# Hybrid encoder layer on Trainium2: one of the two score products of the stick-breaking heads on 64 instead of 128 rows of TensorE

## The chip, the core and the metric

The kernel runs on one core of a Trainium2 chip. The metric is device time of one execution in microseconds (us); lower is better. The engines are called as in the profile: PE is TensorE's matmul side, PEld its weight loads, DVE VectorE, ACT ScalarE, POOL GpSimd, and SP the engine whose queue issues most DMAs.

## What is computed

One encoder layer on a sequence of 2048 positions with 1024 features: a normalisation, a projection to queries, keys and values, two groups of eight heads with 64 features each, an output projection, and an MLP with 4096 hidden features. Only the first group of heads is touched by the change. It is stick-breaking attention, strictly causal, cut here to its core:

```python
z = jnp.einsum('bqhd,bkhd->bhqk', qb, kb).astype(jnp.float32) * scale
strict = s_idx < t_idx
log_beta = jax.nn.log_sigmoid(z)
log_1m_beta = jnp.where(strict, jax.nn.log_sigmoid(-z), 0.0)
suffix = lax.cumsum(log_1m_beta, axis=3, reverse=True) - log_1m_beta
w = jnp.where(strict, jnp.exp(log_beta + suffix), 0.0)
outs.append(jnp.einsum('bhqk,bkhd->bqhd', w.astype(v.dtype), vb))
```

A weight is thus the sigmoid of the score, times the product of the sigmoids of the negated scores of all keys between this key and the query. The second group is softmax attention in a band of keys with a position bias.

## The kernel before

**Numbers in two parts.** PE multiplies operands of type fp32r here. For accuracy each fp32 number is kept as two such parts: the first is the number rounded, the second what the rounding left over (`split`). A product of two matrices is made as first x first, first x second, second x first (`mm3`), added up in PSUM.

**Stages.** Projections of the later half of the sequence come first, to about 420 us. Then comes attention, to about 1360 us, with the rest of the projections and the output projection of finished blocks as filler between its steps. The last stage, the MLP with the remaining output projection, is dense PE work.

**The score tile.** Scores of the heads are made from 64 features, half of PE's 128 rows. The kernel uses the other half for the parts of the keys: `load_k` (line 673) puts the first parts of k on partitions 0 to 63 and the second parts on 64 to 127. `load_q` (line 666) puts the same 64 features of q on both halves; index 0 of its tile is q's first part, index 1 its second. One product over 128 rows therefore gives q's first part times (k's first plus k's second part), and another gives q's second part times the same sum. In `SB.scores` (line 776) the two are added in one PSUM tile `z`, for 128 queries (the loaded weights) by up to 512 keys (the moving columns). In units on the diagonal the keys ahead of the query block are left out, so that 512, 384, 256 or 128 columns remain, and a third product of identity and mask in bf16 writes a large negative number where a key isn't before the query (line 785).

**The steps of a unit.** A unit (`SB`) is a head, a block of 512 queries and a block of 512 keys; there are 80, each with four steps of 128 queries. In a step, `soft1` (line 787) makes two sigmoids on ACT, a running product (scan) along the keys on DVE, and the weights as a product on POOL. Eight steps later (`LAG`, line 1039) the weights are transposed on PE (tiles `wt`), split by ACT and DVE (`wth`, `wtl`), and multiplied with the values (`acc`).

**Order of the work.** PE's order is the program's: all PE calls go through `Ordered`, whose line 42 is therefore the line of nearly all instructions in the profile. The loop at line 1115 goes step by step: transposes of the unit eight steps back, `soft1` of the current step, splits of the transposed weights, products with the values, then the scores of the next step (called ahead by one step), then filler. `fill` (line 1055) gives out filler products (tiles `pf` and `po`) by a credit that grows with the weight of a step, so their share follows the steps and not the clock. Units run from the last query block to the first; in each block the stick-breaking units come ahead of the softmax units. The softmax heads (`CA`) make their scores by the same pair of 128-row products (`cz`, `ct`).

Of the kernel before, what the change touches and what calls it, by code (L numbers as in the profile page):

```python
# [21 lines left out]
HD = 64  # L22
# [57 lines left out]
def encoder_kernel(ctx, tc, xT, c, g1, g2, w_in, w_rest, gqk, bias, w_o, w1, w2, w_ada, b_ada, out):  # L80
    nc = tc.nc
    act, dve, pool, sp = nc.scalar, nc.vector, nc.gpsimd, nc.sync
    pe = Ordered(tc, nc.tensor)
# [572 lines left out]
    if True:  # L656
# [97 lines left out]
        class SB(Unit):  # L754
# [21 lines left out]
            def scores(self, qi):  # L776
                nm = f"{self.nm}_{qi}"
                c0 = qi * P if self.diag else 0
                n = TB - c0
                self.z = z = pz.tile([P, TB], F32, tag="z", name=f"z{nm}")  # L780
                qs = slice(qi * P, (qi + 1) * P)
                pe.matmul(z[:, :n], self.q[:, 0, qs], self.k[:, c0:], start=True, stop=False)
                pe.matmul(z[:, :n], self.q[:, 1, qs], self.k[:, c0:], start=False, stop=not self.diag)
                if self.diag:
                    pe.matmul(z[:, :P], identb, maskb, start=False, stop=True)

# [892 lines left out]
```

## Time and profile before

| | us |
|---|---|
| median of the 2 runs shown | 2668.22 |
| lowest and highest of them | 2667.61, 2668.83 |
| span of the profiled execution | 2672.1 |
| PE busy in it | 2598.4 |
| attention, roughly | 410 to 1360 |
| PE busy in 410 to 1360 | 908.5 of 950 |
| first and last stick-breaking score product | 421.1, 1269.1 |

The span is that of one profiled execution; the profile tells no further time around it, so it stands for that execution's own time, 3.9 us above the median. A row of a group reads: line, engine, operation, output<-inputs by the program's names, shape, count, then busy time in us and the mean duration of one in ns, then the idle time of the engine before these instructions and what ended it. The pair ahead of the shape (128*128) tells the rows and columns of PE that the instruction uses. Busy time counts overlapping instructions once, so busy time over count is nearer to the rate than the duration is. Rows of the timeline read: start in us, length in us, engine, instruction, count, and in brackets an idle time before it. Ends of products are modelled in the records; starts tell the rate.

### The profile page before, as it was taken

The numbers are of one execution on the slowest core, as the hardware profiler recorded it, in microseconds if no ns is written. First come the engines' busy times: TensorE is split into PE (matmuls) and PEld (weight loads), VectorE is DVE, ScalarE is ACT, GpSimd is POOL, SyncE is SP. The second block draws the span as 40 slices with busy tenths as digits, with TensorE's granted clock in tenths as the row PEclk, the third lists the DMA queues.
The fourth block names the chain that finished last, engine by engine and source line by source line (L and its number), as shares of the span: only waits on it lengthen the run. The fifth ranks groups of instructions, "written<-read, shape, count | busy, mean of one in ns | idle before, by whom it ended". The sixth has DMA issues, their size and how long they took to land. (4 is left out here: it accounts for less than half of the span.)

```text
span 2672.1 us, 40291 instructions
## 1 busy us (share of the span) xinstructions
PE 2598.4 (97%) x12944; PEld 2162.5 (81%) x12944; DVE 1929.1 (72%) x3287; ACT 1511.7 (57%) x2962; POOL 919.8 (34%) x1192
## 2 busy tenths in 40 slices
PE   6999999898999999999999999999999999999999
PEld 5888887687878887778788888878888888888887
DVE  7656766698789878989768787677857656555555
ACT  5333436787688878878654444456544545444443
POOL 4330144576467656767522323100002323200000
PEclk9999999999999999999999999999999999999999
DMA  9879888988887687756677777786675343465574
GB/s 339 307 300 363 313 318 261 262 255 258 251 260 249 203 260 251 236 191 206 208 276 274 273 255 266 252 322 221 222 265 175 138 166 140 148 250 197 194 266 156
DMA packets 263061, 651.28 MB, mean 244 GB/s; under 512 B 29632, under 2 KB 61376, under 8 KB 252992
## 3 DMA queue, kind: packets, MB, share of 16 engines
q1 hardware_dynamic: 261552, 643.98, 70.5%
q10 hardware_dynamic: 1296, 4.72, 0.4%
q8 instruction: 103, 1.69, 0.3%
q14 instruction: 110, 0.90, 0.1%
HBM read 457.21 MB, written 191.37 MB: 243 GB/s over the span
## 5 line engine op out<-in xcount | busy, mean ns | idle before, releaser
L42 PE MATMUL ps<-oph,opv 128*128 128x512 f32 x2688 | 612.5, 390 | 0.3
L42 PE MATMUL ps<-h,opw 128*128 128x512 f32 x2664 | 607.0, 390 | 4.3 <-DVE cx L42 4.3
L42 PEld LDWEIGHTS ps<-oph,opv 128*128 128x128 f32 x2688 | 503.8, 188 | 107.0 <-DVE opv L42 1.2
L42 PEld LDWEIGHTS ps<-h,opw 128*128 128x128 f32 x2664 | 500.6, 188 | 110.3 <-DVE cx L42 5.8
L42 POOL TENSOR_TENSOR b<-b,p 128x512 f32<-128x512 f32 (+1 forms) x320 | 360.3, 1126 | 197.9 <-DVE p L42 176.6
L42 DVE TENSOR_TENSOR wtl<-wt,wth 128x512 fp32r<-128x512 f32 (+3 forms) x544 | 290.5, 545 | 52.5 <-ACT wth L42 50.0
L42 ACT CAST wth<-wt 128x512 fp32r<-128x512 f32 (+3 forms) x544 | 257.8, 485 | 118.8 <-PE wt L42 104.0
L42 DVE TENSOR_TENSOR oph<-hw,oph 128x512 fp32r<-128x512 f32 x224 | 156.4, 698 | 220.4 <-ACT oph L42 220.4
L42 ACT CAST oph<-hw 128x512 fp32r<-128x512 f32 x224 | 139.5, 623 | 283.3 <-PE ps L42 267.2
L42 PE MATMUL pt<-w,ht 128*128 128x512 f32 x1248 | 288.7, 391 | 2.2 <-DVE qh L42 2.2
L42 POOL TENSOR_TENSOR ts<-w 128x512 f32<-128x512 f32 x32 | 44.8, 1400 | 668.4 <-DMA w<-in_w_dram 576.7
L42 PEld LDWEIGHTS pt<-w,ht 128*128 128x128 f32 x1248 | 232.8, 188 | 50.5 <-ACT csq L42 2.9
L42 DVE TENSOR_TENSOR_SCAN p<-z,p,zero 128x512 f32<-128x512 f32 x192 | 246.1, 1282 | 34.6 <-ACT z L42 29.2
L42 PE MATMUL acc<-wth,v 128*128 128x512 f32 (+3 forms) x544 | 222.6, 413 | 0.8 <-ACT wth L42 0.8
L42 ACT ACTIVATE b<-z 128x512 f32<-128x512 f32 (+1 forms) x320 | 171.7, 537 | 65.7 <-PE z L42 48.3
L42 PE MATMUL z<-k,q 128*128 128x512 f32 (+3 forms) x640 | 186.5, 373 | 9.7 <-DVE p L42 7.2
L42 POOL TENSOR_TENSOR e<-e,cols 128x640 f32<-128x640 f32 (+4 forms) x128 | 143.2, 1123 | 146.1 <-DVE cols L42 81.3
L42 PE MATMUL acc<-wtl,v 128*128 128x512 f32 (+3 forms) x544 | 187.1, 350 | 0.0
L42 DVE TENSOR_TENSOR opw<-w,opw 128x512 fp32r<-128x512 f32 x127 | 103.8, 819 | 113.1 <-ACT opw L42 113.0
L42 PE MATMUL wt<-ident,b 128*128 128x128 f32 x1088 | 173.3, 275 | 6.8 <-DVE cols L42 5.1
L42 ACT ACTIVATE z<-z 128x512 f32<-128x512 f32 (+1 forms) x320 | 170.4, 532 | 0.0
L42 PEld LDWEIGHTS wt<-ident,b 128*128 128x128 f32 x1088 | 134.8, 142 | 37.9 <-DVE cols L42 6.7
(193 smaller groups left out, 4257.6 us busy)
## 6 DMA issues: line engine op xcount, KB each, us to landing
hw<-scr_hid SPq DMA_DIRECT2D x112, 512.0 KB, 3.9
k<-scr_k SPq DMA_DIRECT2D x272, 128.0 KB, 4.2
v<-scr_v SPq DMA_DIRECT2D x136, 256.0 KB, 4.3
q<-scr_q SPq DMA_DIRECT2D x128, 256.0 KB, 5.4
w<-in_w_dram SPq DMA_DIRECT2D x64, 512.0 KB, 5.2
hw<-scr_s SPq DMA_DIRECT2D x64, 512.0 KB, 4.6
fw<-scr_w SPq DMA_DIRECT2D x28, 1024.0 KB, 7.0
wa<-in_w_ada_dram SPq DMA_DIRECT2D x48, 512.0 KB, 6.3
```

Source lines behind the costliest of these rows:

```text
L42: return lambda *x, **y: self.tc.keep_in_program_order(f(*x, **y))
```

## The change

In `SB.scores`, the second product of each tile takes partitions 0 to 63 alone of both operands: q's second part with k's first part. The lower half of that product, q's second part with k's second part, is no longer computed. The first product, the mask, the loads of q and k on all 128 partitions, and the softmax heads stay as they are.

```diff
                 pe.matmul(z[:, :n], self.q[:, 0, qs], self.k[:, c0:], start=True, stop=False)
-                pe.matmul(z[:, :n], self.q[:, 1, qs], self.k[:, c0:], start=False, stop=not self.diag)
+                pe.matmul(z[:, :n], self.q[0:HD, 1, qs], self.k[0:HD, c0:], start=False, stop=not self.diag)
```

## Prediction

> **What bounds the kernel now.** I read the page of the profile first: busy time by engine, then the groups by shape, which split the page's mixed groups.
>
> ```profile
> PE 2598.4 (97%) x12944; PEld 2162.5 (81%) x12944; DVE 1929.1 (72%) x3287; ACT 1511.7 (57%) x2962; POOL 919.8 (34%) x1192
> ```
>
> TensorE (PE) has work in 97% of the span. That is an average over stages, so the next view is the busy time by stretch, for the stretches in which only stick-breaking units are in front; the changed product occurs nowhere else.
>
> ```profile
> 421.00:481.00 60.00, 55.57 (x324) 43.87 (x322) 45.54 (x86) 47.06 (x119) 38.25 (x70) 0.97 0.93 276
> 527.00:654.00 127.00, 122.76 (x786) 106.14 (x785) 110.02 (x159) 104.32 (x221) 85.37 (x137) 0.99 0.80 247
> 744.00:926.00 182.00, 181.29 (x1157) 157.26 (x1156) 165.06 (x215) 150.42 (x312) 127.00 (x193) 1.00 0.73 232
> 1033.00:1270.00 237.00, 232.58 (x1274) 190.23 (x1273) 213.62 (x262) 192.87 (x381) 179.79 (x259) 0.99 0.68 216
> sum 606.00, PE 592.19 PEld 497.50 DVE 534.24 ACT 494.67 POOL 430.40; mean PE 148.05 PEld 124.37 DVE 133.56 ACT 123.67 POOL 107.60
> ```
>
> The columns after the length are PE, PE's weight loads, DVE, ACT, POOL, the granted clock, DMA share and GB/s. PE is busy 592.2 of 606 us, DVE 534.2 (88%). PE is idle for 13.8 us in all. So nothing on PE is hidden here: a nanosecond more on PE in a step lengthens that step, and up to 72 us of DVE idle time would be what a faster PE could win before DVE bound the stretches.
>
> How many instructions the edit touches, and how long one takes, is in the groups with shapes kept apart:
>
> ```profile
> L42 PE MATMUL z<-k,q 128*128 128x512 f32 x448 | 144.5, 404 | 6.6 <-DVE p L42 6.3 <-DMA k<-scr_k 0.2
> L42 PE MATMUL z<-k,q 128*128 128x384 f32 x64 | 16.7, 342 | 0.0
> L42 PE MATMUL z<-k,q 128*128 128x256 f32 x64 | 13.5, 294 | 1.7 <-DVE cols L42 1.3 <-DVE p L42 0.2
> L42 PE MATMUL z<-k,q 128*128 128x128 f32 x64 | 12.0, 268 | 1.4 <-DVE p L42 0.6 <-DVE sv L42 0.5
> L42 PE MATMUL ps<-oph,opv 128*128 128x512 f32 x2688 | 612.5, 390 | 0.3
> ```
>
> 448 + 64 + 64 + 64 = 640 products in 320 score tiles, two in each; the second of each pair, 320 in all, changes. The last row is the densest stream of the kernel: 612.5 us for 2688 products is 0.228 us each, while one lasts 0.390 us in the records. Each product thus overlaps the next by 0.162 us. That overlap, and the weight load that runs under the product before it, are what the change can spoil.
>
> **The change part by part.** *Removed:* the lower 64 of 128 rows of 320 products, that is, q's second part times k's second part. No instruction goes: 640 products and 640 weight loads stay, and so do all DMAs, waits and PSUM tiles. The moving columns stay at 512, 384, 256 or 128. The rows above show time following columns (404, 342, 294, 268 ns); all are of 128 rows, so no row of the trace prices 64. I take zero for the stream itself. Fewer rows saving something would need PE to do two things at once in one pair, but the products before and after use all 128 rows, so I exclude that gain up to what a quieter array may do to the clock: the granted clock in these stretches is 0.97 to 1.00, and 606 us at, say, 0.99 brought to 1.00 is 6 us. Low end of this term: -6 us; taken: 0.
>
> *Added:* 320 products of another shape, each between products of 128 rows, so 640 changes of shape on PE. The page shows every PE group at 128*128, so the trace has no such change. It has three neighbours that bound its price.
>
> The cheapest neighbour is the mask product, in bf16 between fp32 products, a change of operand type there and back:
>
> ```profile
> 904.17 0.62 PE L42 MATMUL z<-k,q 128*128 128x512 f32 x2
> 904.63 0.23 PE L42 MATMUL z<-maskb,identb 128*128 128x128 bf16 x1
> 904.67 0.96 PE L42 MATMUL pf<-fw,fx 128*128 128x256 f32 x6
> 905.46 0.60 PE L42 MATMUL wt<-ident,b 128*128 128x128 f32 x4
> ...
> 906.62 0.23 PE L42 MATMUL z<-maskb,identb 128*128 128x128 bf16 x1
> 906.66 0.84 PE L42 MATMUL pf<-fw,fx 128*128 128x256 f32 x5
> 907.33 0.28 PE L42 MATMUL wt<-ident,b 128*128 128x128 f32 x1
> ```
>
> From mask to the first transpose is 0.83 us with six filler products and 0.71 us with five, so one filler is 0.12 us and the mask with both changes is 0.83 - 6 x 0.12 = 0.11 us. Eight transposes of the same 128 columns take 0.79 us, from 1347.36 to 1348.15, about 0.10 each:
>
> ```profile
> 1347.36 1.03 PE L42 MATMUL wt<-ident,e 128*128 128x128 f32 x8
> 1348.15 0.42 PE L42 MATMUL acc<-wth,v 128*128 128x384 f32 x1
> ```
>
> So a change of operand type costs 0.01 us for the pair of changes. At that price the edit costs 320 x 0.01 = 3 us. This is the bottom of the range of the term.
>
> The second neighbour is a product whose weights were not loaded under the one before, since PE had been idle:
>
> ```profile
> 900.55 0.63 PE L42 MATMUL z<-k,q 128*128 128x512 f32 x2
> 901.02 0.87 PE L42 MATMUL pf<-fw,fx 128*128 128x256 f32 x6
> ```
>
> ```profile
> 1130.04 0.73 PE L42 MATMUL z<-k,q 128*128 128x512 f32 x2 [0.94 <-DVE p L42]
> 1130.61 0.27 PE L42 MATMUL wt<-ident,b 128*128 128x128 f32 x1
> ...
> 1131.85 0.73 PE L42 MATMUL z<-k,q 128*128 128x512 f32 x2 [0.51 <-DVE p L42]
> 1132.42 0.60 PE L42 MATMUL wt<-ident,b 128*128 128x128 f32 x4
> ```
>
> In the stream, the pair of score products takes 0.47 us from its start to the next product's (900.55 to 901.02). After an idle spell it takes 0.57 us, both times. The 0.10 us more is a weight load that nothing covers. If each change of shape keeps the next weights from loading early, it costs 640 x 0.10 = 64 us.
>
> The dearest neighbour adds the emptying of the array: if the next product may start only when the last has left, the overlap of 0.162 us is lost as well, 0.26 us a change, 640 x 0.26 = 166 us.
>
> Between the ends, 3 and 166 us, I take the middle neighbour. The weights of the next product are loaded into rows that the running product occupies; that works between equal shapes (the stream has 0.228 us a product, less than the 0.390 us of one), and the edit makes the two shapes differ on both sides of 320 products. The mask row speaks for less, but it leaves the rows as they are.
>
> Here a rule can be weighed against these rows. The Trainium skill, TensorEngine Tiling, Key Properties, says that a change of tiling mode, unlike a change of tile, drains TensorE. No run here shows such a change; by that rule the sum would be the dearest neighbour's, an estimate of 166 us. The page also gives no time for the drain.
>
> A second rule stands nearer to the middle: TensorE: Matmul & The Clock Gate, Part 3, in the Trainium skill, says that weight loads overlap running products only where their row groups differ. The trace disagrees for equal shapes, where the loads are hidden in the same rows at 0.228 us a product; for unequal shapes no run here shows it.
>
> *What waits:* nothing is queued differently, but all behind a score tile comes later. The chain is score product, two sigmoids on ACT, scan on DVE, product on POOL, transposes eight steps later; its users have slack while PE is late. What a later PE gives back is its own waits for that chain:
>
> ```profile
> PE z L42 <- DVE p L42: 7.2, 11, 2.3
> ```
>
> That is 7.2 us in 11 waits. Each shrinks by at most one step's delay, 0.20 us: 2 us given back (7.2 at the most).
>
> *The sum,* against the profiled execution of 2672.1 us: 0 + 64 - 2 = +62 us, to 2734. That execution's span is 3.9 us above the median of the runs shown, 2668.2; carried over to it, 2668 + 62 = **2730 us**, +2.3%.
>
> **The rivals.** *Shapes mix freely* (not slower, the other side from my forecast). The place is the weight load ahead of each second score product: if it still runs under the first, and the load after it under the second, each pair stays at 0.47 us from start to start. For it: all changes that the trace has, of operand type and into transposes, cost 0.01 us or so. Against it: none of them changes the rows in use. It gives 2668 plus 0 to 3, so 2668 to 2671 us. My forecast turns into no change that a measurement can tell when the price of a change falls below 0.08 us (53 / 640).
>
> *The array empties* at each change, and then loads. For it: PE is full on both sides, so all of 0.26 us would show; in its favour stands the rule of TensorEngine Tiling cited above. Against it: the end of a product is modelled in the records, so 0.162 us is the most, and part of it may be reading that still goes on early. With some 5 us of PE's waits given back: 2668 + 166 - 5 = 2829 us.
>
> *PE gets quicker.* It would need the 64-row products to shorten the pairs by 0.17 us a tile (53 / 320), nearly all of a 512-column product's 0.228 us. DVE would follow at 88% busy. I see nothing in the trace for it; 2615 us or less. With only the clock's gain, 2662 us.
>
> **How the numbers follow.** Exposed loads 0.36, free mixing 0.33, emptying 0.28, quicker 0.03. The likeliest gives 2730 us; its own range is 2698 (only one change of each two exposed) to 2765 (a third of the overlap lost as well). The range of 8 in 10 reaches from 2662 (free mixing with the clock's gain) to 2829, rounded to 2830, which holds the three cases but leaves out the quicker one and what lies beyond full emptying. About 2% (53 us) is what a measurement of this kernel is asked to tell from no change. Slower by over 2%: all of emptying and 0.29 of the 0.36, so 0.57. Within 2%: free mixing and the other 0.07, so 0.40. Faster: 0.03.
>
> **What would show it.** In the profile after, 320 score products and loads stand at 64*128. My step is right if the pair from start to start grows from 0.47 to about 0.57 us, and the product behind it starts some 0.10 us later than its stream would, with the four stretches growing from 606 to about 668 us while all after 1360 us keeps its length. If the pair stays at 0.47 us and the next product is on time, shapes mix freely. If PE's records show gaps of 0.16 us or more beside each score product, the array empties. The prediction is wrong from the start if the groups still read 128*128, or if the time moves in the last stage, where no changed product runs.

## The result, and the profile after

The changed kernel takes 2762.37 us (median of 2 runs, 2762.04 to 2762.70) against 2668.22 before: 1.0351 times the time, 95% interval 1.0331 to 1.0371, or 94 us more. The profiled execution spans 2760.3 us, 1.7 under its own time of 2762.04, and 88.2 more than the one of before. The two differences disagree because the profiled execution of before was a longer one: its span of 2672.1 us is above both of the times shown. Nor does a span stand for an execution's own time, as was assumed ahead of the prediction; with the same 1.7 us added, that execution took some 2674 us (an estimate).

Busy time by stretch says where. The stretches are cut here at the first and last stick-breaking product of each query block; columns after the length are PE, its weight loads, DVE, ACT, POOL, granted clock, DMA share, GB/s. Before:

```profile
421.00:468.00 47.00, 44.43 (x257) 34.51 (x255) 36.45 (x60) 37.05 (x95) 30.74 (x59) 0.96 0.91 276
526.00:646.00 120.00, 115.56 (x736) 99.50 (x735) 103.92 (x147) 99.89 (x217) 81.82 (x132) 0.99 0.79 246
737.00:926.00 189.00, 185.84 (x1182) 160.52 (x1182) 169.25 (x224) 156.45 (x324) 128.56 (x195) 1.00 0.74 235
1009.00:1269.00 260.00, 253.15 (x1389) 207.05 (x1389) 230.72 (x295) 210.86 (x423) 191.12 (x277) 0.99 0.68 219
sum 616.00, PE 598.98 PEld 501.58 DVE 540.34 ACT 504.25 POOL 432.24; mean PE 149.74 PEld 125.39 DVE 135.08 ACT 126.06 POOL 108.06
```

After:

```profile
421.00:474.00 53.00, 52.17 (x254) 35.73 (x255) 38.22 (x60) 37.27 (x94) 30.94 (x59) 0.94 0.88 257
533.00:668.00 135.00, 133.91 (x737) 97.02 (x736) 106.33 (x148) 101.74 (x217) 82.90 (x133) 1.00 0.71 221
757.00:978.00 221.00, 218.92 (x1183) 158.18 (x1182) 171.42 (x224) 159.56 (x324) 128.47 (x196) 0.99 0.64 201
1062.00:1360.00 298.00, 294.58 (x1387) 199.23 (x1387) 234.23 (x294) 214.43 (x421) 191.60 (x278) 0.99 0.59 190
sum 707.00, PE 699.58 PEld 490.16 DVE 550.20 ACT 513.00 POOL 433.92; mean PE 174.90 PEld 122.54 DVE 137.55 ACT 128.25 POOL 108.48
```

The four stretches grew by 707 - 616 = 91 us: all of the 88.2 us between the two spans, and 3 us over. PE's records cover 100.6 us more; its idle time fell from 17.0 to 7.4 us, so 9.6 us were given back. All other engines do about the same work in the longer time.

The groups of PE after the change, shapes apart (mean ns of one behind the comma):

```profile
L42 PE MATMUL z<-k,q 64*128 64x512 f32 x224 | 111.7, 499 | 0.0
L42 PE MATMUL z<-k,q 128*128 128x512 f32 x224 | 91.0, 406 | 2.9 <-DVE p L42 2.9
L42 PE MATMUL z<-k,q 64*128 64x384 f32 x32 | 14.3, 446 | 0.0
L42 PE MATMUL z<-k,q 64*128 64x256 f32 x32 | 12.4, 387 | 0.0
L42 PE MATMUL z<-k,q 64*128 64x128 f32 x32 | 10.4, 324 | 0.0
L42 PE MATMUL z<-k,q 128*128 128x384 f32 x32 | 11.2, 349 | 0.0
L42 PE MATMUL z<-k,q 128*128 128x256 f32 x32 | 9.5, 296 | 1.1 <-DVE cols L42 1.1
L42 PE MATMUL z<-k,q 128*128 128x128 f32 x32 | 8.1, 253 | 0.0
```

All 320 second products stand at 64*128. One with 512 columns lasts 499 ns in the records where its 128-row partner lasts 406; with 384 columns 446 against 349, with 256 columns 387 against 296. The difference is 91 to 97 ns whichever of these three it is: a fixed sum for each, and no slower stream. With 128 columns it is less, 324 against 253, 71 ns. These durations hold modelled ends; what follows goes by starts.

The groups of the weight loads show where it comes from:

```profile
L42 PEld LDWEIGHTS z<-k,q 128*128 128x128 f32 x320 | 60.8, 190 | 14.7 <-DVE p L42 4.4 <-DVE cols L42 1.3
L42 PEld LDWEIGHTS z<-k,q 64*128 64x128 f32 x320 | 58.9, 184 | 94.9 <-issue 91.3
```

A load of 64 rows takes 184 ns in the records where one of 128 takes 190: half the rows save nearly nothing. Ahead of the 64-row loads the load path stands idle for 94.9 us, 0.30 us each, and 91.3 of these wait for nothing that the records show ("issue"). One non-diagonal step in order of time, first PE, then the loads:

```profile
1131.36 0.34 PE L42 MATMUL acc<-wtl,v 128*128 128x384 f32 x1
1131.53 0.82 PE L42 MATMUL z<-k,q 128*128 128x512 f32 x2
1132.29 0.96 PE L42 MATMUL po<-fx,ow 128*128 128x512 f32 x3
1133.09 0.60 PE L42 MATMUL wt<-ident,b 128*128 128x128 f32 x4
```

```profile
1131.36 0.19 PEld L42 LDWEIGHTS z<-k,q 128*128 128x128 f32 x1
1131.85 0.18 PEld L42 LDWEIGHTS z<-k,q 64*128 64x128 f32 x1 [0.31 <-issue]
1132.28 0.53 PEld L42 LDWEIGHTS po<-fx,ow 128*128 128x128 f32 x3 [0.25 <-issue]
```

The first score product starts at 1131.53. The 64-row weights load at 1131.85, 0.32 us later; in the stream of before, a load starts together with the product ahead of it, and the next product starts 0.23 us after that one. So the load is not covered, and it starts 0.09 us later than the next product would have. The product itself starts with its load in these records and the filler's load follows at 1132.28, 0.43 us on: about 0.105 for the load, 0.23 for the stream, 0.09 more. Then three fillers take 0.80 us (1132.29 to 1133.09) in place of 3 x 0.23 = 0.69: the first filler's load, uncovered again. The step has thus grown by (0.32 - 0.23) + (0.43 - 0.23) + (0.80 - 0.69) = 0.40 us, in two portions of some 0.20, one for each change of rows.

That is one step. PE's order is the same in both kernels, so the two profiled executions can also be laid side by side, product by product, and the time from each start to the next compared. What comes later after the change is the start of

- the second score product, by 28.0 us over 320 tiles (0.09 each);
- what stands behind it: the mask on 128 diagonal tiles by 23.8 us, a filler or transpose on the other 192 by 36.8 us (0.19 each);
- the product after that filler or transpose, by 19.3 us over 191 tiles (0.10 each). On the diagonal the two products behind the mask start as before.

That makes 107.9 us. The other starts come 19 us earlier, mostly after waits, which leaves 88.8 us between the first and the last product.

**Theory 1**, formed from this: a change between 64 and 128 rows, in either direction, lets nothing of the next product begin, its weight load included, until the last product has left PE. It costs 0.09 us of emptying, and 0.105 us of load where that load was covered before. That PE empties is a reading: the records show that the load starts 0.09 us after the next product would have started, at 1131.85, while the modelled end of the running product is near 1131.94 (1131.53 and the 0.406 us of its group). A fixed time for changing the shape would look the same, and no run below tells the two apart. **Theory 2**: the 64-row product itself is slow. **Theory 3**: a 64-row result added in a PSUM tile that a 128-row product has just written must wait for it. **Theory 4**: any use of fewer than 128 rows costs.

### The profile page after: what moved, and what is told of

It reads as the page before. It is cut to its first block, busy times and chain, and to the rows that moved or that the text cites. A ratio compares the mean times of both kernels' runs of the same rounds, so it can differ in the third digit from the quotient of the medians.

```text
span 2760.3 us, 40291 instructions
## 1 busy us (share of the span) xinstructions
PE 2699.3 (98%) x12944; PEld 2152.3 (78%) x12944; DVE 1932.8 (70%) x3287; ACT 1520.2 (55%) x2962; POOL 919.9 (33%) x1192
## 5 line engine op out<-in xcount | busy, mean ns | idle before, releaser
L42 PE MATMUL z<-k,q 128*128 128x512 f32 (+7 forms) x640 | 245.8, 419 | 4.0 <-DVE p L42 2.9
L42 PEld LDWEIGHTS z<-k,q 128*128 128x128 f32 (+1 forms) x640 | 119.7, 187 | 109.6 <-issue 91.3
L42 PE MATMUL po<-fx,ow 128*128 128x512 f32 x576 | 172.7, 415 | 0.0
```

The costliest lines, as they stand in the source:

```text
L42: return lambda *x, **y: self.tc.keep_in_program_order(f(*x, **y))
```

## The experiments

Each is an edit of `SB.scores`; the one for one change a tile also edits `soft1` and the loop that calls them. The code cuts are shortened to the products concerned. Medians are given with those of the kernel before in the same group.

**The yardstick.** The changed kernel unaltered.

> The changed kernel once more, as the yardstick of this group. Every theory expects what was measured: 94 us over the kernel before, about 2762 us.

Measured: 2758.47 us against 2669.95, ratio 1.0333 (1.0318 to 1.0349), 88.5 us more (85 to 93 by the interval, which overlaps the 88 to 99 of the first measurement).

**Both products on 64 rows.**

```diff
-pe.matmul(z[:, :n], self.q[:, 0, qs], self.k[:, c0:], start=True, stop=False)
+pe.matmul(z[:, :n], self.q[0:HD, 0, qs], self.k[0:HD, c0:], start=True, stop=False)
-pe.matmul(z[:, :n], self.q[:, 1, qs], self.k[:, c0:], start=False, stop=not self.diag)
+pe.matmul(z[:, :n], self.q[0:HD, 1, qs], self.k[0:HD, c0:], start=False, stop=not self.diag)
```

> Both score products of each tile on 64 rows; q's first part times k's second part is left out too. Theory 1 (each change between 64 and 128 rows empties PE and uncovers the next weight load): still two changes a tile, so about 2762 us, with 0.23 us from the first to the second product as before. Theory 2 (the 64-row product itself is slow): twice as many of them, 2668 + 2 x 94 = 2856 us. Theory 3 (adding a 64-row result into a PSUM tile that a 128-row product has just written has to wait): no such pair is left, so about 2668 us.

Measured: 2773.17 us, ratio 1.0385 (1.0367 to 1.0402), 103 us more. Its timeline, and then its loads:

```profile
1133.72 0.39 PE L42 MATMUL acc<-wtl,v 128*128 128x512 f32 x1
1134.05 0.73 PE L42 MATMUL z<-k,q 64*128 64x512 f32 x2
1134.71 0.96 PE L42 MATMUL po<-fx,ow 128*128 128x512 f32 x3
1135.51 0.27 PE L42 MATMUL wt<-ident,b 128*128 128x128 f32 x1
```

```profile
1134.04 0.29 PEld L42 LDWEIGHTS z<-k,q 64*128 64x128 f32 x2 [0.37 <-issue]
1134.70 0.53 PEld L42 LDWEIGHTS po<-fx,ow 128*128 128x128 f32 x3 [0.37 <-issue]
```

Twice as many 64-row products cost 15 us more than the yardstick and not 94 more, and without any 64-row product behind a 128-row one in the same tile the loss is still there. Theories 2 and 3 fall. The two 64-row loads run in 0.29 us together, so the second starts under the first product: between equal shapes of 64 rows loads are covered as between those of 128. From first to second product it is not the 0.23 us that I had expected but 0.34, since the record of the first starts with its own uncovered load (0.105). The two changes sit at the ends: 1133.72 to 1134.05 is 0.33 in place of 0.23, the pair takes 0.66 in place of 0.47, three fillers 0.80 in place of 0.69; 0.10 + 0.19 + 0.11 = 0.40 us, as in the changed kernel. I had expected the yardstick's time, not 15 us over it. The price of the step is the same, so these 15 us lie elsewhere. Laid side by side with the yardstick's profiled execution, the starts at the score products and the two products behind them differ by under 1 us in sum; products elsewhere, the same in both kernels, come 9.9 us later, and 4 us are longer waits. The mean granted clock is 0.992 here and 0.995 in the yardstick, which by an estimate (0.003 of 2770 us) is 8 us. Why it was lower stays open.

**96 rows.**

```diff
-pe.matmul(z[:, :n], self.q[:, 1, qs], self.k[:, c0:], start=False, stop=not self.diag)
+pe.matmul(z[:, :n], self.q[0:96, 1, qs], self.k[0:96, c0:], start=False, stop=not self.diag)
```

> The second product on 96 rows instead of 64: 32 rows idle. Theory 1, with the added guess that 96 rows are run in the same shape of the array as 128: no change of shape, 2668 us within 5. If fewer rows than 128 in use are enough to empty PE (theory 4): about 2762 us as with 64 rows.

Measured: 2672.22 us, ratio 1.0009 (0.9999 to 1.0019), no difference.

```profile
L42 PE MATMUL z<-k,q 96*128 96x512 f32 x224 | 88.9, 397 | 0.0
```

```profile
L42 PEld LDWEIGHTS z<-k,q 96*128 96x128 f32 x320 | 60.6, 189 | 8.3
```

The 96-row product lasts 397 ns and not 499, and its loads stand behind 8.3 us of idle time, not 94.9. Here 32 idle rows cost nothing: theory 4 falls. That 96 rows are run in the same shape of the array as 128, and 64 in another, is how theory 1 reads it; the records name rows, not shapes.

**The mask between the products.** Against the changed kernel:

```diff
 pe.matmul(z[:, :n], self.q[:, 0, qs], self.k[:, c0:], start=True, stop=False)
-pe.matmul(z[:, :n], self.q[0:HD, 1, qs], self.k[0:HD, c0:], start=False, stop=not self.diag)
 if self.diag:
-    pe.matmul(z[:, :P], identb, maskb, start=False, stop=True)
+    pe.matmul(z[:, :P], identb, maskb, start=False, stop=False)
+pe.matmul(z[:, :n], self.q[0:HD, 1, qs], self.k[0:HD, c0:], start=False, stop=True)
```

> As the changed kernel, but on the diagonal the mask product stands between the two score products instead of behind them. The number of changes of rows stays two a tile. If the mask's own weight load was never covered (as its records before and after the change suggest), the change behind the 64-row product now uncovers a filler's or transpose's load in place of the mask's: 128 tiles x 0.105 = 13 us over the changed kernel, 2775 us. If each change has one price wherever it stands: 2762 us.

Measured: 2770.61 us, ratio 1.038 (1.0364 to 1.0396): 12 us over the yardstick, between 4 and 21 by the ends of the two intervals. In the changed kernel a diagonal step with four fillers takes 792.68 - 790.87 = 1.81 us from first score product to first transpose:

```profile
790.87 0.83 PE L42 MATMUL z<-k,q 128*128 128x512 f32 x2
791.63 0.23 PE L42 MATMUL z<-maskb,identb 128*128 128x128 bf16 x1
791.67 1.17 PE L42 MATMUL pf<-fx,fw 128*128 128x512 f32 x4
792.68 0.60 PE L42 MATMUL wt<-ident,b 128*128 128x128 f32 x4
```

With the mask between, it takes 794.72 - 792.86 = 1.86 us:

```profile
792.86 0.40 PE L42 MATMUL z<-k,q 128*128 128x512 f32 x1
793.10 0.23 PE L42 MATMUL z<-maskb,identb 128*128 128x128 bf16 x1
793.26 0.49 PE L42 MATMUL z<-k,q 64*128 64x512 f32 x1
793.68 1.20 PE L42 MATMUL pf<-fx,fw 128*128 128x512 f32 x4
794.72 0.49 PE L42 MATMUL wt<-ident,b 128*128 128x128 f32 x3
```

That is 0.05 us, 6 us for 128 tiles, half of what I expected from the mask's load. The two profiled executions, both at a granted clock of 0.995, say the same: 2763.6 us here, 2757.4 of the yardstick, 6.2 apart. The other executions here had clocks of 0.992 to 0.994 where the yardstick's had 0.996; 0.003 of 2770 us are 8 us, so by this estimate the clock covers the rest of the 12. The direction holds (a mask behind the 64-row product shares part of the price), the size does not, and why it is half stays open. That the mask's load was uncovered before the change too shows in the load path of the kernel before, ahead of the mask at 904.63:

```profile
904.62 0.10 PEld L42 LDWEIGHTS <-identb 128*128 128x128 bf16 x1 [0.27 <-issue]
```

So with all 128: the load starts 4 ns ahead of its mask, where in the densest stream it starts 223 ns ahead of its product (medians).

**Four changes a tile, and the control for it.** The control, in place of the two score products:

```diff
+for a, b in ((0, n // 2), (n // 2, n)):
+    pe.matmul(z[:, a:b], self.q[:, 0, qs], self.k[:, c0 + a : c0 + b], start=True, stop=False, skip_group_check=True)
+    pe.matmul(
+        z[:, a:b], self.q[:, 1, qs], self.k[:, c0 + a : c0 + b],
+        start=False, stop=not self.diag, skip_group_check=True,
+    )
```

With 64 rows, the second call takes `self.q[0:HD, 1, qs]` and `self.k[0:HD, ...]`. Both return other results than the kernel before, and alike; the likely reason, which was not followed up, is that the accumulation of the second half starts ahead of the mask in the same tile. Products, shapes and order are as described.

> Control, all products on 128 rows as before, but each score product is made in two halves of its columns, in the order first part, second part, first part, second part. No change of rows. Two products of 256 columns take 0.236 us in place of 0.228 for one of 512, and halves of 128 and 64 columns are held up by the weight loads at some 0.11 us each: about 320 x 0.02 to 320 x 0.1, 2675 to 2700 us by every theory.

> As the control, with the second parts on 64 rows: four changes of rows a tile in place of two, and the same columns in all. Theory 1 (price by the number of changes): over the control 192 x 0.78 + 128 x 0.675 = 236 us by the records, less what PE's waits give back and less the loads of the shortest halves that are uncovered in the control already: 190 to 230 us over it. A price by the columns that run on 64 rows (theory 2 in its form of a slow stream): 94 us over the control.

Measured: control 2678.68 us against 2669.44, ratio 1.0038 (1.0025 to 1.0051); with 64 rows 2881.64 us, ratio 1.0802 (1.0761 to 1.0842). The difference is 203 us (190 to 218 by the ends of the intervals), twice the 94 us of the changed kernel for twice the changes, with as many columns on 64 rows as there. Here the four products of a tile take 1212.08 - 1210.93 = 1.15 us, where the control has 0.48 (1112.03 to 1112.51):

```profile
1210.93 1.22 PE L42 MATMUL z<-k,q 128*128 128x256 f32 x4
1212.08 0.50 PE L42 MATMUL po<-fx,ow 128*128 128x512 f32 x1
```

```profile
1112.03 0.63 PE L42 MATMUL z<-k,q 128*128 128x256 f32 x4
1112.51 0.23 PE L42 MATMUL z<-maskb,identb 128*128 128x128 bf16 x1
```

(The rows name the first shape of the four alone.)

**One change a tile, and the control for it.** The scores of two steps are made at once:

```diff
+for z, qs, c0, n in two:
+    pe.matmul(z[:, :n], self.q[:, 0, qs], self.k[:, c0:], start=True, stop=False)
+for z, qs, c0, n in two:
+    pe.matmul(z[:, :n], self.q[0:HD, 1, qs], self.k[0:HD, c0:], start=False, stop=not self.diag)
```

The control has 128 rows in the last call.

> Control, all products on 128 rows as before, but the scores of two steps are made at once: first parts of both tiles, second parts of both, masks of both. No change of rows. Work is the same; the first sigmoid of a pair waits longer and PSUM holds one tile more: 2668 to 2690 us by every theory.

> As the control, with the second parts on 64 rows: two changes of rows for two tiles, half as many as in the changed kernel, and the same 320 products on 64 rows. Theory 1: 96 x 0.389 + 64 x 0.284 = 56 us by the records, less what the waits give back: 40 to 56 us over the control. Theory 2 (the 64-row product itself): 94 us over it. Theory 3 (a 64-row result added to a fresh 128-row one): the first second part comes one product later, so 47 to 94 us.

Measured: control 2693.06 us, ratio 1.008 (1.0065 to 1.0095); with 64 rows 2735.54 us, ratio 1.0243 (1.0225 to 1.026). The difference is 42 us (35 to 52 by the ends of the intervals): half of the loss for half the changes, with the same 320 products on 64 rows. Theory 3's 47 us lies inside that interval; it fell with both products on 64 rows. The control was 3 us dearer than its range: the other order costs 24 us by itself. In its profile the transposes wait 6.1 us for the scan, against 1.0 before; the rest is not traced.

**Other rows.** The second product on 32 rows (`self.q[0:32, 1, qs]`, `self.k[0:32, c0:]`), and on rows 64 to 127 (`self.q[HD:P, 1, qs]`, `self.k[HD:P, c0:]`).

> The second product on 32 rows: the other 32 features of q's second part times k's first part are left out. Theory 1: two changes of shape a tile as with 64 rows, 2755 to 2775 us. If the price follows the rows that stand idle (96 in place of 64): 94 x 96 / 64 = 141, about 2809 us. If fewer rows in use empty sooner, below 2750 us.

> The second product on rows 64 to 127 in place of 0 to 63: q's second part times k's second part is made, times k's first part left out. Theory 1: the same two changes a tile, 2755 to 2775 us. If the price is one of the upper rows (results of 64 rows having to pass the idle lower half, or not): another time by more than 10 us.

Measured, against 2668.22 us: 32 rows 2763.93, ratio 1.0354 (1.0335 to 1.0374); rows 64 to 127 2767.59, ratio 1.0365 (1.0348 to 1.0383). Both are within 10 us of the yardstick's 2758.47, and inside theory 1's range. In the profiled executions the starts at the score products and the two products behind them differ from the yardstick's by under 1 us in sum with 32 rows and by under 3 with rows 64 to 127; what more there is lies elsewhere, at clocks of 0.992 against 0.995. Neither the number of rows (64 or 32) nor their place matters.

## Why the prediction came out as it did

The forecast was 2730 us, in a range of 2662 to 2830; measured were 2762. The sign, the place and the count of two changes a tile were right; the size of the likeliest case, +62 us, was two thirds of the +94 measured. That 2762 still lies in the likeliest case's own range, 2698 to 2765, is partly luck. Its upper end allowed for a third of the overlap, 0.05 us a change, where 0.09 were found; with 0.09 and all else as forecast the sum would be 2668 + 640 x 0.19 - 2 = 2788. Two errors the other way, told below, brought the time back.

- *The stream of 64 rows costs what that of 128 costs: right.* The starts show it: with both products on 64 rows, the second follows the first by 338, 281 and 224 ns at 512, 384 and 256 columns, on 128 rows before by 233, 177 and 119, so 104 or 105 ns more whatever the columns, the uncovered load.
- *640 changes of shape on a full PE, each showing in the time: right.* The four stretches grew by 91 us, against the 62 forecast, and four, two and one change a tile cost 203, 94 and 42 us.
- *Between the neighbours I took the uncovered load alone, 0.10 us a change: this is the step that failed.* The load is uncovered, at about the size that I read from the products behind an idle spell. But each change costs a further fixed wait, read here as the emptying of the array, which the sum had at nothing and a rival held. What the runs show is that rival with a smaller size: 0.09 us in place of the 0.162 by which records of products overlap. The overlap is a modelled end, and I had named that as the rival's weak point without letting it lower its price.
- *Not all changes pay both.* In the changed kernel's diagonal tiles the mask follows the 64-row product, and the product after the mask is on time: mask to first filler is 0.04 us (791.63 to 791.67), as before the change. Emptying at 640 changes and newly uncovered loads at 640 - 128 = 512 make 640 x 0.09 + 512 x 0.105 = 111 us, close to the 107.9 us by which the starts come later, and to the 101 by which PE's records grew. I had counted the load 640 times. The mask between the products confirmed only half of the mask's part.
- *The mask row as a cheap change (0.01 us): misread.* I compared it with transposes of 128 columns, which took some 0.10 us each though 128 columns of the stream are 0.228 / 4 = 0.06 us. Products that short are held by something else, by all signs their weight loads: in the control with halves, products of 128 and of 64 columns alike start 0.11 us apart. The mask's 0.11 us therefore was no cheap change. Its load was uncovered already, as the row shown with the mask between the products tells. It bounded the range from below and did no harm, but it gave free mixing a chance of 0.33 that the row didn't support.
- *Waits given back, 2 us (7.2 at the most): too low.* PE's idle time in the stretches fell by 9.6 us. I had counted one kind of wait only, that of score products for the scan; that one fell from 7.2 to 2.9 us.
- *The rule of the Trainium skill, TensorEngine Tiling, Key Properties,* that a change of tiling mode drains TensorE and a change of tile doesn't, agrees with these runs if a change between 128 and 64 rows is such a change of mode: 0.09 us at each change, none between two 64-row products, and none for 96 rows. The drain itself is in no record.
- *The other rule cited, of the Trainium skill, TensorE: Matmul & The Clock Gate, Part 3,* that loads overlap only where row groups differ, does not agree with these runs: two products on the same 64 rows have their second load covered (0.29 us for both loads).

## What to carry to other kernels

In a full PE stream, count the changes between shapes of the array, not the idle rows: each cost some 0.2 us of PE's time here, nearly the 0.23 of a product with 512 columns. Rows that the product doesn't need are best left in the shape of their neighbours, as the kernel before does, or the products of one shape put next to each other. And when a row of a trace seems to price a change cheaply, check first what else bounds that row.

## What the runs showed of the hardware that was not expected

- 96 rows run beside 128 at no cost (ratio 1.0009, 0.9999 to 1.0019), while 64 and 32 rows in its place cost 88 to 99 us over 320 products.
- A load of 64 rows takes 184 ns in the records, one of 128 rows 190.
- The wait at a change is the same whatever the columns of the product that leaves: the 64-row product starts 91 to 94 ns later behind its 128-row partner than the 128-row one did before (medians for 512, 384, 256 and 128 columns).
- A load for a product of another type, bf16 among fp32, was not covered before the change either: the mask's 128 loads start 4 ns ahead of their masks, those of the densest stream 223 ns ahead of their products.
